# Encoder step on one core: a mixing paced anew, squares in another bank, copies on another engine, one evacuation behind two blocks

## The chip, the cores and the metric

The kernel runs on one core of a Trainium2 chip. The metric is device time in microseconds (us) of one execution; lower is better. TensorE multiplies matrices into PSUM banks; VectorE, ScalarE and GpSimd work on the data around it; SyncE issues most DMAs. In the profile TensorE is PE (its weight loads PEld), VectorE DVE, ScalarE ACT, GpSimd POOL, SyncE SP.

## The reference

One step of a streaming encoder with two layers for T = 1056 positions (1024 of a new stream, 32 of a running one) of width 1024, in float32. The even layer, which the change touches, reads:

```
h    = rms_norm(x, g_pre)
z    = h @ w_in                      # a | u | v | gate
y_a  = pool_mixer(a)                 # trailing means, a small matmul per group
v    = layer_norm(gelu(v));  u = gelu(u)
mix_ = W_s (128 x 128, masked, per head) applied over each chunk of 128 positions of v, + b_s
y_b  = u * mix_
y    = (concat(y_a, y_b) * silu(gate)) @ w_out
x    = x + rms_norm(y, g_post)
```

The odd layer starts with another rms_norm and a projection with w2, then does latent attention. The last piece of the change lies in that projection.

## The kernel before

Data lie transposed: 128 channels on the partitions, positions along the free axis. A tensor of 1024 channels is eight blocks. The 1056 positions are split into half a (640, computed as two pieces of 320 into a two-bank PSUM tile `za`) and half b (416, into a bank `zb`). Each float32 product is three matmuls of a rounded form (fp32r): high by high, high by low, low by high, in `mm_block` (L115). So each weight block has a high part, cast on ScalarE (L150), and a low part, the difference (L151, on GpSimd or VectorE), both made in `prep_w` from a raw block that SyncE loads; and each operand has such a pair. `za`, `zb` and `mi` have two buffers each, `whi` and `wlo` four, `raw` three.

The part that matters is the output projection of the even layer, in `even`. Its operand has sixteen blocks of channels: `mix[0..7]` (pool mixer times gate) and `mix[8..15]` (gating mixer times gate), the latter made from the tiles `mB[0..7]`, which lie in l8 to l15.

- First loop, m = 0 to 7: the product with `mix[0..7]`, half a for all m, half b only for m in BOTH = (0, 3, 4, 5). `put` (L678) copies the results to `yp[m]` with ScalarE (L679 from za, L681 from zb).
- While it runs, the mixing over positions goes on beside it. `sgu_task` starts nine tasks `sgu(t)`, one for each 128 positions. Each casts its piece of v (L743 on ScalarE, L744 on VectorE), and then for q = 0 to 3 sends a group of four small matmuls into an `mi` bank (in the trace `mi<-r,r`), reads it with VectorE (L763, L764, twice each) and multiplies the result into two blocks of mB with GpSimd (L766). Tiles 0 to 4 are half a.
- After the first loop, tasks are stepped until five tiles are done; then `split_a` (L781) casts the eight blocks of mB for half a: high part on ScalarE (L785), low part on VectorE (L786).
- Second loop, m = 0 to 7, half a: the product with `mix[8..15]`, added to `yp` (L827); the squares of the sum go into two banks (L831, ScalarE) and are summed up (L833, VectorE) for the norm that follows.
- Half b of w_out: twelve jobs in the order m = 6, 7, 1, 2 (two jobs each, low half and high half of the sixteen blocks), 0, 3, 4, 5 (one job each). The result is added to `yp[m].b` (L854) or, for 6, 7, 1, 2, copied there (L856); squares follow (L858, L860). The residual of half a runs beside it: `residual` (L863) with L884, L885, L896 on VectorE, L888 (a DMA), L895 and, for the squares, L289 on ScalarE and L290 on VectorE.
- `odd_in` (L911): w2 for half a in blocks 0 to 5, each followed by an evacuation on VectorE (`evac`, L192) that multiplies by rstd of half a's second norm; then half b. `rstd` (L198) sums over channels with small matmuls (L209), computes on VectorE (L216) and GpSimd (L217 to L219), spreads the result (L227, matmuls into `mi`, L240). For half b, L907 adds up the squares before it.

What sets the order: TensorE's order is the order of the program. Tasks are generators; each is due at a time of a pacing clock that advances by a fixed count with each matmul, and after each step over k `mm_block` takes one step of the task that is most overdue (`poll`). The table `N` (L35) holds the delays: "sg" ahead of the mixing's first task, "lead" from one tile to the next, "mix" between a tile's casts and its first group, "mixq" from group to group. The order on the other engines is made by a scheduler. The lines at the end of the first loop:

```
        while len(done) < 5:
            self.step(min(self.tasks, key=lambda t: t[:2]))
        split_a()
```

Of the kernel before, what the change touches and what calls it, by code (L numbers as in the profile page):

```python
# [23 lines left out]
NA, NB, CA = 640, 416, 320  # L24
# [7 lines left out]
        "kn e 2": 4.31, "v p 2": 5.302, "kn o 0": 6.344, "qn o 0": 6.796, "v p 3": 7.31, "v p 4": 8.3,  # L32
        "kn o 1": 8.827, "qn o 1": 10.546, "kn o 2": 12.035, "qn o 2": 12.785}

N = {"ld0": 18000, "ld": 8500, "tp": 5500, "sa": 9000, "sl": 12000, "sb": 6000, "sbk": 2000, "sg": 3000, "x": 462, "mix": 5000, "mixq": 2450, "tr": 717, "lead": 9800, "tr0": 11989, "res": 9194, "ra": 2699,  # L35
     "rb": 1574, "ha": 8000, "hb": 5000, "kv": 429, "q": 20908, "k": 34682, "kvs": 1773, "qs": 10662, "rest": 1357, "r1": 1608,
     "r2": 1337, "fa": 5400, "tn": 1800, "w0": 2000, "w1": 1552, "f0": 1645, "f1": 626, "fy": 648}
HF = 6
# [34 lines left out]
def two(ap):  # L73
    return ap.rearrange("p (c n) -> p c n", c=2)


class Build:
# [122 lines left out]
    def rstd(self, acc, g, dim, out, scale=None, wait=None):  # L200
# [14 lines left out]
        for w, c0, c1 in spans:  # L215
# [3 lines left out]
            nc.gpsimd.tensor_tensor(rl[:w, c0:c1], m[:w, c0:c1], rh[:w, c0:c1], ALU.subtract)  # L219
        yield (wait or (N["w0"], N["w1"]))[0]  # L220
        rep = None
        for c0 in range(0, len(widths), 2):
            ws = widths[c0 : c0 + 2]
            dh, dl = (self.t(self.cst, [P, 256], F32R, n) for n in ("dgh", "dgl"))
            for d, r in ((dh, rh), (dl, rl)):
                for e, w in enumerate(ws):
                    nc.vector.tensor_scalar(d[:w, e * P : e * P + w], self.ident[:w, :w], r[:w, c0 + e : c0 + e + 1],  # L227
                                            None, ALU.mult)
            yield (wait or (N["w0"], N["w1"]))[1]
            if c0 % 4 == 0:  # L230
# [88 lines left out]
    def even(self):  # L319
        nc = self.nc  # L320
# [27 lines left out]
        def split_x(g, k):  # L348
            x = xs[k][:, :NA] if g == "a" else xs[k][:, NA:T]
            hi, lo = h[k][0].get(g), h[k][1].get(g)  # L350
            nc.scalar.activation(hi, x, AF.Copy, scale=self.vec(GA1, k))
            nc.vector.scalar_tensor_tensor(lo, x, self.vec(GA1, k), hi, ALU.mult, ALU.subtract)
            return x
# [20 lines left out]
        def t_prep():  # L374
            for k in range(4):
                q = [[xs[k + 4 * i][:, j * HT : (j + 1) * HT] for j in range(2)] for i in range(2)]
                for i in range(2):
                    nc.scalar.activation(xs[k + 4 * i][:, :T], xs[k + 4 * i][:, :T], AF.Copy, scale=self.vec(GA1, k + 4 * i))
                tt = nc.vector.tensor_tensor
                tt(q[0][0], q[0][1], q[0][0], ALU.subtract)  # L380
                tt(q[0][1], q[1][1], q[0][1], ALU.subtract)
                tt(q[1][1], q[1][1], q[0][0], ALU.subtract)
                tt(q[1][0], q[1][0], q[1][1], ALU.subtract)
                for j, i in enumerate(((9, 10), (0, 4), (1, 5), (2, 6))[k]):
                    tl[2 * k + j] = R(i, F32R)
                for n, (j, e, o, f) in place.items():
                    hi, lo = X[n](k)
                    src = xs[k + o][:, f * HT : (f + 1) * HT]
                    nc.scalar.copy(hi, src)
                    tt(lo, src, hi, ALU.subtract)  # L390
                yield N["tp"]

# [6 lines left out]
        for g in "ab":  # L399
            acc, *sqs = (v[:, mpos[g]] for v in sums)  # L400
            z = [(zt[0], None), (zt[1], None)] if g == "a" else [(None, zt[2][:, i, :]) for i in range(2)]
            for k in range(NK):
                x = split_x(g, k)
                for i in range(2):
                    self.mm_block(self.wcol(wts[8 + i]), h, [k], g, ps=z[i], first=k == 0, last=k == 7)
                self.sumsq(acc, x, k == 0, g, nc.vector, sqs[k % 2])
            self.spawn(self.rstd(acc, g, D, rep.get(g)), N["x"])
            if g == "a":
# [78 lines left out]
        for g, z in (("a", zz), ("b", z)):  # L487
# [3 lines left out]
            if g == "a":  # L491
                tp = self.spawn(t_prep(), N["tp"])
            for i in range(2):
                ps = (zt[i], None) if g == "a" else (None, zt[2][:, i, :])
# [15 lines left out]
        def lead_task():  # L510

            for t in range(9):
# [12 lines left out]
                if t == 8:  # L525
                    w = R(13)
                    for e in range(2):
# [6 lines left out]
                        nc.scalar.dma_start(self.o_sv[:, o], lg)  # L534
                yield N["ld"]

# [24 lines left out]
        for p, (b0, b1) in enumerate(pairs):  # L561
# [13 lines left out]
            else:  # L575
                for e in range(2):
                    i = (b0, b1)[e] % 8
# [11 lines left out]
        mix = {}  # L589
# [12 lines left out]
        def pool_evac(blk, ps):  # L602
            a = pslot("a")
            nc.gpsimd.memset(a[:, 0:16], 0.0)
            nc.gpsimd.tensor_copy(a[:, 1040:1056], hist[:, blk, :])
            nc.vector.tensor_tensor(two(a[:, 16 : 16 + NA]), ps[0][:, :, :CA], two(rep.a), ALU.mult)
            nc.vector.tensor_tensor(a[:, 656:1040], ps[1][:, :384], rep.b[:, :384], ALU.mult)
            nc.vector.tensor_tensor(a[:, 1056:1088], ps[1][:, 384:NB], rep.b[:, 384:], ALU.mult)
            return a
# [40 lines left out]
        for i, blk in enumerate(A_ORDER):  # L650
# [5 lines left out]
            ps = self.mm_block(self.wcol(wts.pop(blk)), h, range(NK))  # L656
# [4 lines left out]
            a = pool_evac(blk, ps)  # L661
# [142 lines left out]
        for m in range(2, NK):  # L804
# [5 lines left out]
            ps = self.mm_block(self.wcol(w), mix, A_ORDER, "ab" if m in BOTH else "a")  # L810
# [7 lines left out]
        for m in range(NK):  # L818
            if m < 7:
                wn = self.prep_w(self.i_wout[m + 1, :, 1024:], lo_on=nc.vector)  # L820
            else:
                wA = self.prep_w(self.i_wout[6, :, :1024], lo_on=nc.vector)
            ps = self.mm_block(lambda k: self.wcol(wB)(k - 8), mix, range(8, 16), "a")
            if m < 7:
                wB = wn
            y = yp[m].a
            nc.vector.tensor_tensor(two(y), two(y), ps[0][:, :, :CA], ALU.add)  # L827
            for c in range(2):
                yc, ac = two(y)[:, c], two(acc)[:, c]
                sq = ac if m == 0 else self.bank("zb")[:, :CA]  # L830
                nc.scalar.activation(sq, yc, AF.Square)  # L831
                if m:
                    nc.vector.tensor_tensor(ac, ac, sq, ALU.add)  # L833
# [7 lines left out]
        for j, (m, c) in enumerate(jobs):  # L841
            if j + 1 < len(jobs):
                mm, cc = jobs[j + 1]
                wn = self.prep_w(self.i_wout[mm, :, cc * 1024 : cc * 1024 + 1024], lo_on=nc.vector)
            if c == 0:
                ps = self.mm_block(self.wcol(w), mix, A_ORDER, "b", last=False)
                w = wn
                continue
            ps = None if m in BOTH else ps
            ps = self.mm_block(lambda k: self.wcol(w)(k - 8), mix, range(8, 16), "b", ps=ps, first=ps is None)  # L850
            w = wn
            y = yp[m].b
            if m in BOTH:
                nc.vector.tensor_tensor(y, y, ps[1][:, :NB], ALU.add)  # L854
            else:
                nc.vector.tensor_copy(y, ps[1][:, :NB])  # L856
            sq = self.bank("za")[:, 0, :NB]
            nc.scalar.activation(acc if m == order[0] else sq, y, AF.Square)  # L858
            if m != order[0]:
                nc.vector.tensor_tensor(acc, acc, sq, ALU.add)  # L860
# [50 lines left out]
    def odd_in(self):  # L911
        nc = self.nc
# [3 lines left out]
        z = self.yp[:6]  # L916

        def block(i, groups, ps=None):
            w = wts.pop(i)
            if i + 1 < len(seq):  # L920
                wts[i + 1] = self.prep_w(self.i_w2[seq[i + 1]])
            return self.mm_block(self.wcol(w), h2, range(NK), groups, ps=ps)

        for b in range(6):
            ps = block(b, "a")
            while "a" not in self.reps or any(t is self.reps["a"] for t in self.tasks):
                self.step(min(self.tasks, key=lambda t: t[:2]))
            rep2 = self.rep2
            self.evac(ps, z[b], rep2, "a")
        while any(t is self.res for t in self.tasks):  # L930
            self.step(self.res)

# [2 lines left out]
        pss = [block(6 + b, "b", (None, zs[b])) for b in range(4)]  # L935
# [76 lines left out]
        for m in range(8):  # L1012
            ps = block(12 + m, "ab")
# [469 lines left out]
```

## Time and profile before

| | us |
|---|---|
| median of three runs | 1308.68 |
| lowest and highest | 1307.97, 1315.05 |
| profiled execution, its own time | 1318.26 |
| its span in the trace | 1316.2 |
| TensorE busy | 1265.5 (96%) |
| VectorE busy | 865.6 (66%) |
| ScalarE busy | 552.0 (42%) |
| GpSimd busy | 304.9 (23%) |

The profile is of one execution, slower by 9.6 us than the median. Positions in it are us from the start of its span. A timeline's row gives start, length, engine, line, operation, output <- inputs, shapes, the number of instructions taken together, and in brackets the idle time of the engine ahead of it with what ended that. Matmuls overlap, so from one to the next the starts are compared. [...]

### The profile page before, as it was taken

To read this page: it belongs to the slowest core of one execution; us is meant where nothing else is said; L and a number is where in the kernel's file an instruction comes from. 1 tells how busy PE (TensorE), PEld (TensorE's weight loads), DVE (VectorE), ACT (ScalarE), POOL (GpSimd) and SP (SyncE) were. 2 spreads that over 40 slices of the span, in tenths; PEclk is the share of its full clock that TensorE was granted. 3 is DMA by queue.
4 is the path that set the end of the run, shared out by engine and by line. 5 is a ranking of instruction groups with operands and counts; after the bars stand their busy time and mean duration, and the time that the engine had idled before them with its cause. 6 is when DMAs were issued, how large, how long until landed. Compare 5 with 4: busy or idle time off the path is not lost.

```text
span 1316.2 us, 22118 instructions
## 1 busy us (share of the span) xinstructions
PE 1265.5 (96%) x8488; PEld 1232.0 (94%) x8488; DVE 865.6 (66%) x1620; ACT 552.0 (42%) x1035; POOL 304.9 (23%) x381
## 2 busy tenths in 40 slices
PE   9899999999999999999998999999999999999995
PEld 8899989999999999989997989999999999998993
DVE  7977668886768764478578824733667666665438
ACT  8643432343422223243344423424556565654431
POOL 0200000000033332443102444222223332322410
PEclk9899999999999999989999989998999999999998
DMA  6022346522233253222355333222111111116425
GB/s 226 10 89 98 99 154 209 196 69 88 95 110 107 65 187 126 73 78 88 125 167 177 105 117 115 95 82 66 47 44 46 48 46 52 46 53 198 160 88 193
DMA packets 77562, 139.40 MB, mean 106 GB/s; under 512 B 10736, under 2 KB 33712, under 8 KB 77456
## 3 DMA queue, kind: packets, MB, share of 16 engines
q1 hardware_dynamic: 57776, 105.57, 25.5%
q10 hardware_dynamic: 19680, 32.42, 6.8%
q8 instruction: 67, 1.10, 0.3%
q14 instruction: 39, 0.32, 0.1%
HBM read 101.74 MB, written 36.21 MB: 105 GB/s over the span
## 4 chain that ended last, share of the span: by engine, by line
PE 79%; DVE 11%; DMA 4%; issue 3%; ACT 1%; POOL 1%; ACTq 0%; SPq 0%; DVEq 0%; POOLq 0%
PE za L115 20%; PE z L115 18%; PE sc L115 12%; PE pj L115 12%; PE zb L115 11%; PE pj L1157 2%; PE mi L115 2%; DMA r<-vd 1%; DVE wlo L447 1%; DMA r<-in_w 1%; PE mi L209 1%; DVE wlo L151 1%; PE mi L549 1%; DVE a L1380 1%; DVE r L907 1%
## 5 line engine op out<-in xcount | busy, mean ns | idle before, releaser
L115 PE MATMUL z<-l,whi 128*128 128x264 f32 (+2 forms) x1312 | 248.9, 296 | 9.6 <-DVE r L192 2.1
L150 ACT CAST whi<-raw 128x512 fp32r<-128x512 f32 (+1 forms) x180 | 108.3, 604 | 309.9 <-PE zb L115 134.9
L151 POOL TENSOR_TENSOR wlo<-raw,whi 128x512 fp32r<-128x512 f32 (+2 forms) x122 | 157.0, 1289 | 296.1 <-ACT whi L150 290.9
L115 PEld LDWEIGHTS z<-l,whi 128*128 128x128 f32 x1312 | 197.3, 191 | 12.9 <-DVE r L477 2.5
L115 PE MATMUL z<-l,wlo 128*128 128x264 f32 (+2 forms) x880 | 187.6, 292 | 2.6 <-DVE wlo L447 2.6
L115 PE MATMUL za<-a,whi 128*128 128x320 f32 x704 | 145.2, 313 | 0.9 <-DVE r L641 0.9
L115 PEld LDWEIGHTS z<-l,wlo 128*128 128x128 f32 x880 | 140.0, 191 | 3.2 <-DVE wlo L447 3.1
L115 PEld LDWEIGHTS za<-a,whi 128*128 128x128 f32 x704 | 117.4, 190 | 1.6 <-ACT whi L150 1.2
L115 PE MATMUL za<-l,whi 128*128 128x320 f32 (+1 forms) x496 | 112.2, 316 | 0.0
L115 PEld LDWEIGHTS za<-l,whi 128*128 128x128 f32 x496 | 90.8, 191 | 0.7
L1130 POOL TENSOR_SCALAR p<-p,nm 128x128 f32<-128x128 f32 (+8 forms) x72 | 53.0, 736 | 164.5 <-DVE nm L1129 129.1
L115 PE MATMUL z<-r,whi 128*128 128x264 f32 x448 | 90.6, 284 | 0.0
L115 PE MATMUL za<-a,wlo 128*128 128x320 f32 x352 | 80.6, 310 | 0.0
L115 PE MATMUL zb<-l,whi 128*128 128x416 f32 x224 | 76.4, 353 | 0.0
L115 PE MATMUL zb<-b,whi 128*128 128x416 f32 x224 | 72.4, 358 | 1.9 <-DVE rep L833 1.9
L1128 ACT ACTIVATE p<-sc,nm 128x128 f32<-128x128 f32 (+8 forms) x72 | 50.6, 703 | 45.1 <-DVE nm L1127 31.9
L115 PEld LDWEIGHTS z<-r,whi 128*128 128x128 f32 x448 | 69.3, 188 | 0.0
L446 ACT CAST whi<-r 128x512 fp32r<-128x512 f32 x56 | 34.7, 621 | 77.3 <-PE z L115 60.9
L115 PEld LDWEIGHTS za<-a,wlo 128*128 128x128 f32 x352 | 62.0, 190 | 0.2
L447 DVE TENSOR_TENSOR wlo<-r,whi 128x512 fp32r<-128x512 f32 x56 | 38.4, 685 | 30.5 <-ACT whi L446 30.5
L115 PE MATMUL za<-l,wlo 128*128 128x320 f32 (+1 forms) x248 | 58.1, 313 | 0.0
L115 PE MATMUL sc<-a,whi 128*128 128x400 f32 x256 | 57.6, 346 | 0.2 <-ACT p L1128 0.2
(317 smaller groups left out, 3049.5 us busy)
## 6 DMA issues: line engine op xcount, KB each, us to landing
raw<-in_w SPq DMA_DIRECT2D x64, 256.0 KB, 2.7
r<-in_w SPq DMA_DIRECT2D x56, 256.0 KB, 2.8
raw<-in_wout SPq DMA_DIRECT2D x56, 256.0 KB, 3.1
mBd<-r ACTq DMA_DIRECT2D x8, 528.0 KB, 2.8
gAd<-r ACTq DMA_DIRECT2D x8, 528.0 KB, 3.5
l<-mBd SPq DMA_DIRECT2D x8, 528.0 KB, 5.8
vd<-r ACTq DMA_DIRECT2D x16, 256.0 KB, 2.9
r<-vd SPq DMA_DIRECT2D x8, 512.0 KB, 4.3
```

What stands on the lines that cost most here:

```text
L115: self.nc.tensor.matmul(out, lhsT, rhs, start=start, stop=stop)
L150: nc.scalar.copy(hi[:, :m], raw[:, :m])
L151: (lo_on or nc.gpsimd).tensor_tensor(lo[:, :m], raw[:, :m], hi[:, :m], ALU.subtract)
L209: nc.tensor.matmul(st[:w, j : j + 1], acc[:, j * P : j * P + w], self.one, start=True, stop=True)
L446: nc.scalar.copy(hi, src)
L447: lo_on.tensor_tensor(lo, src, hi, ALU.subtract)
L549: nc.tensor.transpose(pt[:n, j * 256 + e * P : j * 256 + (e + 1) * P], d[e][:, i * P : i * P + n], self.ident)
L907: nc.vector.tensor_tensor(acc2, acc2, sq, ALU.add)
L1128: nc.scalar.activation(pv, view, AF.Exp, bias=nm[:n, 0:1], accum_out=nm[:n, 1:2])
L1130: nc.gpsimd.tensor_scalar(p[:n, :K], p[:n, :K], nm[:n, 2:3], 1.0, ALU.mult, ALU.mult)
L1157: nc.tensor.transpose(tr[:, e, :], p[:, (b + e) * P : (b + e + 1) * P], self.ident)
L1380: nc.vector.scalar_tensor_tensor(y[m], y[m], self.vec(GP2, m), rep, ALU.mult, ALU.mult)
```

## The change

Four edits. The pacing delays "sg", "mix" and "lead" are shorter. In the second loop's last block the squares of half a are written to the `mi` bank instead of `zb`. The copies of L856 are made by ScalarE. In `odd_in` the evacuation of block 0, and with it the loop that steps tasks until rstd is there, stands behind block 1 in the program.

```diff
--- before.py
+++ after.py
@@ -32,7 +32,7 @@
         "kn e 2": 4.31, "v p 2": 5.302, "kn o 0": 6.344, "qn o 0": 6.796, "v p 3": 7.31, "v p 4": 8.3,
         "kn o 1": 8.827, "qn o 1": 10.546, "kn o 2": 12.035, "qn o 2": 12.785}
 
-N = {"ld0": 18000, "ld": 8500, "tp": 5500, "sa": 9000, "sl": 12000, "sb": 6000, "sbk": 2000, "sg": 3000, "x": 462, "mix": 5000, "mixq": 2450, "tr": 717, "lead": 9800, "tr0": 11989, "res": 9194, "ra": 2699,
+N = {"ld0": 18000, "ld": 8500, "tp": 5500, "sa": 9000, "sl": 12000, "sb": 6000, "sbk": 2000, "sg": 0, "x": 462, "mix": 3200, "mixq": 2450, "tr": 717, "lead": 9000, "tr0": 11989, "res": 9194, "ra": 2699,
      "rb": 1574, "ha": 8000, "hb": 5000, "kv": 429, "q": 20908, "k": 34682, "kvs": 1773, "qs": 10662, "rest": 1357, "r1": 1608,
      "r2": 1337, "fa": 5400, "tn": 1800, "w0": 2000, "w1": 1552, "f0": 1645, "f1": 626, "fy": 648}
 HF = 6
@@ -827,7 +827,7 @@
             nc.vector.tensor_tensor(two(y), two(y), ps[0][:, :, :CA], ALU.add)
             for c in range(2):
                 yc, ac = two(y)[:, c], two(acc)[:, c]
-                sq = ac if m == 0 else self.bank("zb")[:, :CA]
+                sq = ac if m == 0 else self.bank("mi" if m == 7 else "zb")[:, :CA]
                 nc.scalar.activation(sq, yc, AF.Square)
                 if m:
                     nc.vector.tensor_tensor(ac, ac, sq, ALU.add)
@@ -853,7 +853,7 @@
             if m in BOTH:
                 nc.vector.tensor_tensor(y, y, ps[1][:, :NB], ALU.add)
             else:
-                nc.vector.tensor_copy(y, ps[1][:, :NB])
+                nc.scalar.copy(y, ps[1][:, :NB])
             sq = self.bank("za")[:, 0, :NB]
             nc.scalar.activation(acc if m == order[0] else sq, y, AF.Square)
             if m != order[0]:
@@ -921,12 +921,17 @@
                 wts[i + 1] = self.prep_w(self.i_w2[seq[i + 1]])
             return self.mm_block(self.wcol(w), h2, range(NK), groups, ps=ps)
 
+
+        pss = []
         for b in range(6):
-            ps = block(b, "a")
+            pss.append(block(b, "a"))
+            if b == 0:
+                continue
             while "a" not in self.reps or any(t is self.reps["a"] for t in self.tasks):
                 self.step(min(self.tasks, key=lambda t: t[:2]))
             rep2 = self.rep2
-            self.evac(ps, z[b], rep2, "a")
+            for i in (0, 1) if b == 1 else (b,):
+                self.evac(pss[i], z[i], rep2, "a")
         while any(t is self.res for t in self.tasks):
             self.step(self.res)
```

How instructions move. First TensorE, at the start of the second loop, in the kernel before; `mi_...` are groups of the mixing, `za_755` is block 0 of the second loop (another group, mi_739, stands directly ahead of these rows):

```order
L115 MATMUL mi_744_6205<-r5_638_5464,r1_722_6063 128x256
L115 MATMUL mi_744_6205<-r5_638_5464,r3_723_6064 128x128
L115 MATMUL mi_744_6205<-r5_638_5464,r1_722_6063 128x256
L115 MATMUL mi_744_6205<-r5_638_5464,r3_723_6064 128x128
L115 MATMUL mi_746_6217<-r5_638_5464,r1_722_6063 128x256
L115 MATMUL mi_746_6217<-r5_638_5464,r3_723_6064 128x128
L115 MATMUL mi_746_6217<-r5_638_5464,r1_722_6063 128x256
L115 MATMUL mi_746_6217<-r5_638_5464,r3_723_6064 128x128
L115 MATMUL za_755_6258<-r6_641_5471,whi_726_6083 128x320 x2
L115 MATMUL za_755_6258<-r7_642_5472,whi_726_6083 128x320 x2
```

Three groups stand back to back there, between block 7 of the first loop and block 0 of the second. The same place in the changed kernel, from the last matmul of block 7 (`za_739`) on:

```order
L115 MATMUL za_739_6142<-a6_616_5349,wlo_717_6016 128x320 x2
L115 MATMUL mi_747_6221<-r5_638_5464,r1_722_6033 128x256
L115 MATMUL mi_747_6221<-r5_638_5464,r3_723_6034 128x128
L115 MATMUL mi_747_6221<-r5_638_5464,r1_722_6033 128x256
L115 MATMUL mi_747_6221<-r5_638_5464,r3_723_6034 128x128
L115 MATMUL za_756_6263<-r6_641_5471,whi_734_6131 128x320 x2
L115 MATMUL za_756_6263<-r7_642_5472,whi_734_6131 128x320 x2
L115 MATMUL za_756_6263<-r6_641_5471,wlo_735_6132 128x320 x2
L115 MATMUL za_756_6263<-a0_469_4461,whi_734_6131 128x320 x2
L115 MATMUL za_756_6263<-a1_471_4463,whi_734_6131 128x320 x2
L115 MATMUL za_756_6263<-a0_469_4461,wlo_735_6132 128x320 x2
L115 MATMUL mi_758_6283<-r5_638_5464,r2_740_6161 128x256
```

One group is left between the blocks; mi_744 and mi_745 (a group of the sixth tile) now lie inside block 7, and mi_758, the sixth tile's second, inside block 0.

Next VectorE in the changed kernel, up to the last row that reads mi_745 (a... are the split blocks of `mix`, l12 and l13 blocks of mB, dgh, dgl and tm temporaries):

```order
L763 SCALAR_TENSOR_TENSOR dgh_746_6214<-mi_744_6180,vecs_5_69,r8_639_5469 128x128
L764 SCALAR_TENSOR_TENSOR dgh_746_6214<-mi_744_6180,vecs_5_69,dgh_746_6214 128x128
L786 TENSOR_TENSOR a7_524_4791<-l12_631_5445,a6_522_4789 128x640
L763 SCALAR_TENSOR_TENSOR tm_757_6276<-mi_745_6203,vecs_5_69,r8_639_5469 128x128
L786 TENSOR_TENSOR a1_563_5051<-l13_632_5446,a0_561_5049 128x640
L764 SCALAR_TENSOR_TENSOR tm_757_6276<-mi_745_6203,vecs_5_69,tm_757_6276 128x128
L151 TENSOR_TENSOR wlo_755_6259<-raw_753_6257,whi_754_6258 128x512
L763 SCALAR_TENSOR_TENSOR dgl_748_6226<-mi_747_6221,vecs_5_69,r8_639_5469 128x128
L763 SCALAR_TENSOR_TENSOR tm_757_6276<-mi_745_6203,vecs_5_69,r8_639_5469 128x128
L764 SCALAR_TENSOR_TENSOR dgl_748_6226<-mi_747_6221,vecs_5_69,dgl_748_6226 128x128
L763 SCALAR_TENSOR_TENSOR dgl_748_6226<-mi_747_6221,vecs_5_69,r8_639_5469 128x128
L764 SCALAR_TENSOR_TENSOR tm_757_6276<-mi_745_6203,vecs_5_69,tm_757_6276 128x128
```

The reads of mi_744, mi_745 and mi_747 now stand among L786 of `split_a` and two L151 of the weights; before, the L151 stood behind all L786.

Last, ScalarE in the changed kernel, around the copy of the fourth of the blocks that L856 copies (l2; l5 is half a's residual):

```order
L888 DMA x1d_6_74<-l5_597_5228 128x640
L895 ACTIVATE a2_954_7416<-l5_597_5228,vecs_5_69 128x640
L289 ACTIVATE a8_896_7121<-l5_597_5228 128x640
L856 COPY l2_594_5225<-zb_943_7343 128x416
L150 CAST whi_958_7436<-raw_957_7435 128x512
L858 ACTIVATE za_956_7432<-l2_594_5225 128x416
L150 CAST whi_961_7442<-raw_960_7441 128x512
```

and VectorE in the kernel before, at the same copy:

```order
L290 TENSOR_TENSOR a7_895_7120<-a7_895_7120,a8_896_7121 128x640
L885 TENSOR_TENSOR l5_597_5228<-l5_597_5228,a5_893_7118 128x640
L856 COPY l2_594_5225<-zb_943_7343 128x416
L151 TENSOR_TENSOR wlo_959_7437<-raw_957_7435,whi_958_7436 128x512
L151 TENSOR_TENSOR wlo_962_7443<-raw_960_7441,whi_961_7442 128x512
L884 SCALAR_TENSOR_TENSOR l6_598_5229<-l6_598_5229,vecs_5_69,a6_894_7119 128x640
```

The copy stood behind L885 of l5 on VectorE; it now stands on ScalarE behind L895 and L289 of l5.

From TensorE's L209 of the second norm of half a on, no instruction of any engine changes its place against another of the same engine; that holds for all blocks of `odd_in`.

## Rows read from the trace of the kernel before

**Rows 1.** The page, part 1: busy us, share of the span, instructions.
```profile
PE 1265.5 (96%) x8488; PEld 1232.0 (94%) x8488; DVE 865.6 (66%) x1620; ACT 552.0 (42%) x1035; POOL 304.9 (23%) x381
```

**Rows 2.** TensorE's waits, 480 to 800 us: operand or bank awaited, total, times, longest.
```profile
PE mi L209 <- DVE r L907: 5.2, 1, 5.2
PE zb L115 <- DVE rep L833: 1.9, 1, 1.9
PE mi L115 <- DVE tm L764: 1.8, 1, 1.8
PE zb L115 <- DVE l L854: 1.6, 2, 1.3
PE mi L115 <- DVE dgh L764: 1.4, 1, 1.4
PE mi L115 <- DVE dgh L227: 1.1, 1, 1.1
PE mi L115 <- DVE dgl L227: 1.0, 1, 1.0
PE zb L115 <- DVE l L856: 1.0, 1, 1.0
```

**Rows 3.** Stretches: length, busy us of PE, PEld, DVE, ACT, POOL, granted clock, DMA.
```profile
580.00:586.00 6.00, 5.94 (x24) 5.97 (x25) 5.70 (x11) 3.99 (x6) 2.50 (x5) 0.52 0.03 11
597.00:647.00 50.00, 50.00 (x346) 49.12 (x346) 38.83 (x96) 18.11 (x34) 12.53 (x28) 1.00 0.24 67
650.00:654.00 4.00, 3.98 (x13) 3.81 (x14) 0.36 (x1) 0.13 (x1) 0.00 (x0) 0.57 1.04 397
671.00:711.00 40.00, 37.38 (x193) 35.27 (x192) 37.91 (x57) 22.37 (x36) 1.99 (x1) 1.00 0.68 213
760.00:766.30 6.30, 6.19 (x25) 6.16 (x26) 2.64 (x9) 0.74 (x1) 1.92 (x6) 0.50 0.41 145
```

**Rows 4.** TensorE's timeline, 566 to 576: start us, us, engine, line, what.
```profile
567.21 0.75 PE L115 MATMUL za<-a,whi 128*128 128x320 f32 x4
...
568.09 0.57 PE L115 MATMUL mi<-r,r 128*128 128x256 f32 x4
568.50 0.80 PE L115 MATMUL za<-a,whi 128*128 128x320 f32 x4
...
575.63 0.57 PE L115 MATMUL mi<-r,r 128*128 128x256 f32 x4
```

**Rows 5.** VectorE's timeline at the end of the mixing.
```profile
577.37 0.81 DVE L786 TENSOR_TENSOR a<-l,a 128x640 fp32r<-128x640 f32 x1
...
579.31 0.34 DVE L764 SCALAR_TENSOR_TENSOR dgh<-mi,vecs,dgh 128x128 f32<-128x128 f32 x1
579.57 0.34 DVE L764 SCALAR_TENSOR_TENSOR tm<-mi,vecs,tm 128x128 f32<-128x128 f32 x1
...
581.73 1.04 DVE L786 TENSOR_TENSOR a<-l,a 128x640 fp32r<-128x640 f32 x1
```

**Rows 6.** VectorE's timeline at the end of the second loop.
```profile
642.12 0.68 DVE L151 TENSOR_TENSOR wlo<-raw,whi 128x512 fp32r<-128x512 f32 x1
642.72 0.88 DVE L833 TENSOR_TENSOR rep<-rep,zb 128x320 f32<-128x320 f32 x2
```

**Rows 7.** GpSimd's timeline at the end of the mixing.
```profile
577.52 0.97 POOL L766 TENSOR_TENSOR l<-l,dgh 128x128 f32<-128x128 f32 x1 [1.42 <-DVE dgh L764]
...
581.63 0.46 POOL L766 TENSOR_TENSOR l<-l,dgh 128x128 f32<-128x128 f32 x1 [1.03 <-DVE dgh L764]
```

**Rows 8.** ScalarE's timeline there.
```profile
582.54 0.73 ACT L785 CAST a<-l 128x640 fp32r<-128x640 f32 x1
```

**Rows 9.** VectorE's timeline in half b of w_out.
```profile
695.03 0.59 DVE L856 COPY l<-zb 128x416 f32<-128x416 f32 x1
695.53 0.69 DVE L151 TENSOR_TENSOR wlo<-raw,whi 128x512 fp32r<-128x512 f32 x1
```

**Rows 10.** ScalarE's timeline in the first loop of w_out.
```profile
509.31 0.51 ACT L681 COPY l<-zb 128x416 f32<-128x416 f32 x1
```

## The prediction

> **What bounds the kernel now.** The busy table comes first: TensorE is busy 96% of the span, every other engine 66% or less [rows 1]. So the end is set by TensorE's own work and by the holes in it, and an edit that leaves the matmuls alone can only take holes away or make new ones. The list of TensorE's waits between 480 and 800 us, which covers all that the change touches, is therefore read next [rows 2]: each row is a hole, with the instruction that ended it. [...]
>
> [...]
>
> **A**, the end of the mixing over positions: 1.4 + 1.8 = 3.2 us of waiting for L764 [rows 2], then 6 us at a mean clock of 0.52 [rows 3]. Work that goes at 0.52 for 6 us would have taken 3.1 us, so the tail costs 2.9. Together 6.1.
>
> **B**, before half b of w_out: 1.9 us for L833 [rows 2], then 4 us at 0.57, a tail of 0.43 x 4 = 1.7. Together 3.6.
>
> **C**, inside half b of w_out: 1.0 us for L856 and 1.6 for L854 [rows 2] = 2.6. Their stretch was granted 1.00 [rows 3], so there is no tail.
>
> **D**, rstd of half a's second norm: 1.1 and 1.0 us for L227 [rows 2].
>
> **E**, rstd of half b's second norm: 5.2 us for L907 [rows 2] and a tail of 0.5 x 6.3 = 3.2. It is the largest, 8.4 us, and the change's last rows on each engine lie well ahead of it; I leave it as it is.
>
> **Edit 1, the pace of the mixing (place A).** Before, the last three groups of `mi` matmuls stand back to back behind block m=7 (first order fence). There are two `mi` buffers, so the second and third each wait until VectorE has read an older one: that is A. In the change three groups move into the blocks, and one more (tile 5's first) goes ahead of the second loop; behind block 7 only mi_747 is left, and mi_758 comes after two steps over k of the second loop's block 0 (second fence).
>
> TensorE's side: a step takes 568.09 - 567.21 = 0.88 us and a group 568.50 - 568.09 = 0.41 [rows 4]. Before, block 7 ended at 575.63 [rows 4]; with three more groups ahead of that it ends at 575.63 + 3 x 0.41 = 576.86. mi_747 takes it to 577.27, and after two steps, at 579.03, mi_758 is wanted.
>
> VectorE's side: mi_758 takes over the buffer of mi_745, which is free when the last row of the third fence has read it. In VectorE's order, from the first read of mi_744 (three rows ahead of that fence) up to there, stand 11 of L763/L764, 2 of L786 and 2 of L151. L763 and L764 follow each other at 579.57 - 579.31 = 0.26, an L786 takes 0.81 [rows 5], an L151 642.72 - 642.12 = 0.60 [rows 6]: 2.86 + 1.62 + 1.20 = 5.7 us. The run begins when mi_744 is there, four steps and one group before 576.86, at 572.93, and two L786 in front of it are done, 1.62 later: 574.55. One hole lies in it: the first L786 needs its l12 multiplied on GpSimd (0.46 us [rows 7]) and cast on ScalarE (0.73 [rows 8]) after an L764, 1.2 us in which VectorE has two rows (0.52) to do: 0.7 idle. The end is 574.55 + 5.7 + 0.7 = 580.95, with a semaphore's 0.1 about 581.1. So mi_758 **waits 2.1 us**. No row shows this wait, so it is bounded: 0 if VectorE comes into block 7 with no arrears, and about 3.2 (the whole of A's present waiting) if its L786 are stretched. I take 2.1, by the walk. A wait of 1.9 had a tail of 1.7 at B, and waits of 1.0 to 1.3 had none at C [rows 2, 3]; 2.1 is nearest to B, so I add 1.7. A comes to 3.8 in place of 6.1: **-2.3 us**.
>
> All nine tiles start earlier as well. From 597 to 647, VectorE is busy 38.83 of 50 us [rows 3], so it has room and I price that at 0; if it has none, see the last rival.
>
> **Edit 2, m=7's squares (place B).** Both zb buffers hold squares of the last block, and half b's first block waits for L833, the last reader. With the squares in `mi` it needs the zb of block 6's squares, read by the L833 at 642.72 [rows 6], seven us earlier. Its weights' last low part is L151 at 642.12 [rows 6]; nothing else is late. `mi` has no other user until the next rstd, in half b's third job, so the other bank costs nothing. Wait and tail go: **-3.6 us**. Next late would be the weights of the job after, which are cast as soon as this one gives its buffers back, and so move with it.
>
> **Edit 3, four copies to ScalarE (place C).** From 671 to 711 VectorE is busy 37.91 of 40 us [rows 3]: there it is the bound, some 5 us behind TensorE, and each zb buffer comes free when VectorE gets to it. A copy occupies it from 695.03 to 695.53, 0.50 us [rows 9]. Four that leave bring all behind them forward by **2.0 us**, and TensorE with them; the rest of C's 2.6, about 0.6, stays as smaller waits for L854. ScalarE takes 0.51 us for such a copy out of zb (the same in put()) [rows 10], at 22.37 of 40 busy [rows 3]: hidden. But its order matters: the copy of l2 stands behind L895 and L289 of l5 (fourth fence), which themselves wait for VectorE's L885 of l5. That row stands a few places earlier now, so I expect the copy done by about 694. TensorE wants the buffer 1.0 us [rows 2] before the copy of today ends (695.03 + 0.59), at 694.6. Bounds: 0 if it is late all the same, 2.6 if all three waits go.
>
> **Edit 4, block 0's evac.** TensorE's rstd rows already lay inside block 0, and on every engine the instructions of odd_in stand in the same sequence as before: the edit does not do what its code says, and I give it 0 from both sides. **D** keeps its 2.1: GpSimd's order ahead of that rstd is the same; one of its two waits, 1.1, may go or come again, and I use that for the range.
>
> **Sum.** -2.3 - 3.6 - 2.0 = -7.9 us, against the profiled execution's own 1318.26: 1310.4. That execution is 9.6 us above the median shown, 1308.68, with the same program; I take the difference over unchanged: **1300.8**.
>
> **Rivals.**
> (1) *A goes clean.* VectorE is ahead, mi_758 waits under 1 us, no tail. For it: VectorE was only 66% busy overall. Against it: 5.7 us of VectorE's work must fit in the 4.5 us from 574.55 to 579.03. -6.1 - 3.6 - 2.0 = -11.7: 1297.0.
> (2) *A is given back whole.* Where an L786 started beside GpSimd's L766 (581.63) it took 1.04 us in place of 0.81, and where GpSimd started second (577.52) its L766 took 0.97 in place of 0.46 [rows 5, 7]. Denser mixing makes such meetings more frequent. Five L786 in the walk times 0.23 = 1.2 more waiting: 3.3 with A's present tail of 2.9 is 6.2, against 6.1 now. The sum is then -5.6: 1303.1. [...]
> (3) *C gives nothing.* The copy of l2 comes out no earlier, since L885 of l5 is held in VectorE's queue: -2.3 - 3.6 = -5.9: 1302.8. With (2) as well: -3.6, 1305.1.
> (4) *Slower: the second loop cannot hold the new pace.* A tile comes every 9.0 in place of 9.8 of the pacing clock. If VectorE is full there, each of three later tiles waits like A now, 2.1 + 2.9 = 5.0: 15 in place of 6.1, +8.9 - 5.6 = +3.3: 1312.0. It decides once VectorE's share of the loop passes 100%; it is 78% now [rows 3], and 78 x 9.8/9.0 is 85. That speaks against it.
> (5) *An edit does nothing.* For edit 4 that is part of the forecast.
>
> **How the numbers follow.** Forecast 0.50; (1) 0.16; (2) 0.16; (3) 0.10; (4) 0.05; others 0.03. A measurement of this kernel can tell about 0.5%, 6.5 us, from no change: the line is at 1302.1. The forecast is 1.3 us below it, with errors of 1 to 2, so a quarter of its chance counts as no change: 0.37 and 0.13. Faster: 0.37 + 0.16 + 0.03 of (2) = 0.56. Same: 0.13 + 0.13 of (2) + 0.10 + 0.02 = 0.38. Slower: 0.05 + 0.01 = 0.06. The range goes from (1) with all of C (1296.4) less one wait of D, 1295.3, to (2) and (3) together, 1305.1, plus one wait of D, 1306.2.
>
> **What would show it.** A wait of about 2 us of an `mi` matmul for L764 in the second loop's block 0, with a granted clock near 0.5 behind it, in place of the two ahead of the loop; no wait for L833, and a clock of 1.00 where half b starts; zb waits between 690 and 712 under 1 us in sum; the waits for L227 and L907 as before, the last still 5 us with its tail. Wrong would be: new waits in the second loop (rival 4), an unchanged wait for l2's copy, now on ScalarE (3), or a changed E, which I hold fixed.

## The result and the profile after

| | before | changed |
|---|---|---|
| median, us | 1309.62 (4 runs) | 1301.99 (4 runs) |
| lowest to highest | 1307.97 to 1315.05 | 1299.84 to 1302.51 |
| span of the profiled execution | 1316.2 | 1298.0 |

The ratio of the changed kernel's time to the other's is 0.9922, 95% interval 0.9899 to 0.9945: 10.2 us off 1309.6, between 7.2 and 13.2. The medians in the table are 7.6 apart, inside that interval. The prediction was -7.9 us, 1300.8 with a range of 1295.3 to 1306.2, and faster at 0.56.

The spans differ by 18.2 us, more than the medians, since they are single executions. The traced one of the changed kernel is the fastest of its four (mean granted clock, as a share of TensorE's full clock, 0.991; the others 0.987 to 0.989 and 1.9 to 2.7 us longer), and that of the kernel before, 1318.26 us, is slower than every run in the table. So a stretch is cut out that both traces share: it begins at the `za` matmul that waits 0.9 us for L641, shortly ahead of the first row that the change moves, and ends at half b's L209, behind the last. First the kernel before, then the changed one, TensorE's timeline:

```profile
500.21 0.82 PE L115 MATMUL za<-a,whi 128*128 128x320 f32 x4 [0.89 <-DVE r L641]
```

```profile
760.11 1.64 PE L209 MATMUL mi<-one,r 128*128 128x1 f32 x8 [5.19 <-DVE r L907]
```

```profile
496.23 0.82 PE L115 MATMUL za<-a,whi 128*128 128x320 f32 x4 [0.88 <-DVE r L641]
```

```profile
746.41 1.63 PE L209 MATMUL mi<-one,r 128*128 128x1 f32 x8 [5.20 <-DVE r L907]
```

From start to start that is 259.90 us before and 250.18 in the changed kernel: **9.7 us** gone inside the stretch. The rest, 4.0 ahead of it and 4.5 behind, lies where nothing was changed.

TensorE's waits in the changed kernel, 480 to 800 us, as in [rows 2]:

```profile
PE mi L209 <- DVE r L907: 5.2, 1, 5.2
PE mi L115 <- DVE tm L764: 2.2, 1, 2.2
PE mi L115 <- DVE dgl L227: 1.0, 1, 1.0
...
PE zb L115 <- DVE wlo L151: 0.3, 1, 0.3
PE mi L115 <- DVE dgh L227: 0.3, 1, 0.3
PE zb L115 <- ACT whi L150: 0.2, 1, 0.2
PE mi L115 <- DVE dgh L764: 0.2, 1, 0.2
```

The two waits of A have become one of 2.2 and one of 0.2, L833 (B) is gone, no wait for L854 or L856 is left (C), only 0.3 and 0.2 for weights; L907 (E) stands as it was. The stretches, columns as in [rows 3]:

```profile
576.00:580.00 4.00, 1.93 (x14) 1.96 (x15) 4.00 (x10) 1.46 (x3) 3.14 (x4) 1.00 0.21 66
580.00:586.00 6.00, 6.00 (x45) 6.00 (x44) 5.77 (x14) 2.36 (x5) 1.85 (x4) 1.00 0.45 131
...
640.00:650.00 10.00, 10.00 (x55) 9.88 (x55) 4.30 (x7) 3.45 (x7) 0.00 (x0) 1.00 0.85 293
...
746.40:752.70 6.30, 6.29 (x30) 6.26 (x31) 2.54 (x8) 1.34 (x2) 1.91 (x6) 0.62 0.38 133
```

The 2.2 us end at 578.07, and the stretches around it and behind were granted 1.00: no tail, as a stretch of lower clock behind a wait is called, at A, where [rows 3] had 0.52 for 6 us. Half b's start, at 640.7, has 1.00 as well. VectorE did not become idle in half b of w_out: from half b's first matmul to half a's L209 it is busy 46.56 of 57.45 us, against 46.74 of 61.47 before; the four copies are gone from it, and a few rows that lay ahead of it or behind it have come in. Behind E the clock is still low, 0.62 in the mean.

The last rows of the third order fence as they ran, on VectorE, and the matmul that they release:

```profile
571.41 0.34 DVE L763 SCALAR_TENSOR_TENSOR dgh<-mi,vecs,r 128x128 f32<-128x128 f32 x1
...
573.95 0.83 DVE L786 TENSOR_TENSOR a<-l,a 128x640 fp32r<-128x640 f32 x1 [0.69 <-ACT a L785]
...
574.95 0.81 DVE L786 TENSOR_TENSOR a<-l,a 128x640 fp32r<-128x640 f32 x1
...
577.58 0.34 DVE L764 SCALAR_TENSOR_TENSOR tm<-mi,vecs,tm 128x128 f32<-128x128 f32 x1
```

```profile
578.07 0.65 PE L115 MATMUL mi<-r,r 128*128 128x256 f32 x4 [2.21 <-DVE tm L764]
```

From the first read of mi_744 (571.41) to the end of the last of mi_745 (577.92) it took 6.5 us, 0.69 of it idle for ScalarE's cast; the walk through VectorE's rows in the prediction had 5.7 + 0.7. The matmul starts 0.15 us behind that end, where the walk had 0.1 for the semaphore. ScalarE around the fourth copy:

```profile
682.14 0.83 ACT L895 ACTIVATE a<-l,vecs 128x640 fp32r<-128x640 f32 x1 [1.59 <-DVE wlo L151]
682.87 0.72 ACT L289 ACTIVATE a<-l 128x640 f32<-128x640 f32 x1
683.50 0.48 ACT L856 COPY l<-zb 128x416 f32<-128x416 f32 x1
```

L895 and L289 of l5 do stand in front of it; it ends at 683.98, and TensorE, which needs that bank next, starts at 684.56 after a wait of 0.22 us for weights. Their cast (L150, 683.89 to 684.51) is the row behind the copy on ScalarE.

### The profile page after: what moved, and what is told of

It reads as the page before. It is cut to its first block, busy times and chain, and to the rows that moved or that the text cites. A ratio compares the mean times of both kernels' runs of the same rounds, so it can differ in the third digit from the quotient of the medians.

```text
span 1298.0 us, 22126 instructions
## 1 busy us (share of the span) xinstructions
PE 1255.4 (97%) x8488; PEld 1222.3 (94%) x8488; DVE 862.1 (66%) x1616; ACT 552.5 (43%) x1039; POOL 306.4 (24%) x381
## 4 chain that ended last, share of the span: by engine, by line
PE 79%; DVE 11%; DMA 4%; issue 3%; ACT 2%; POOL 1%; ACTq 0%; SPq 0%; DVEq 0%; POOLq 0%
PE za L115 20%; PE z L115 18%; PE sc L115 12%; PE pj L115 11%; PE zb L115 11%; PE pj L1162 2%; PE mi L115 2%; DMA r<-vd 1%; DVE wlo L447 1%; DVE wlo L151 1%; PE mi L209 1%; PE mi L549 1%; DVE r L907 1%; DVE a L1385 1%; DVE l L884 1%
## 5 line engine op out<-in xcount | busy, mean ns | idle before, releaser
L150 ACT CAST whi<-raw 128x512 fp32r<-128x512 f32 (+1 forms) x180 | 107.9, 603 | 290.1 <-PE zb L115 121.2
L151 POOL TENSOR_TENSOR wlo<-raw,whi 128x512 fp32r<-128x512 f32 (+2 forms) x122 | 157.8, 1296 | 289.0 <-ACT whi L150 285.4
```

Source lines behind the costliest of these rows:

```text
L150: nc.scalar.copy(hi[:, :m], raw[:, :m])
L151: (lo_on or nc.gpsimd).tensor_tensor(lo[:, :m], raw[:, :m], hi[:, :m], ALU.subtract)
```

## The experiments

The first four start from the changed kernel and put back one edit each. Ratios are to the kernel before, as timed on the same chip; the changed kernel has 0.9922, and the one with block 0's evacuation put back, which runs the same, 0.9911, so 0.9917 is taken for it. Worked out from the two intervals, that is known to about 0.0013, so a run that differs from it by less than some 0.0025 is not told apart by the ratio alone. One thousandth is 1.3 us. "The stretch" is the one from the wait for L641 to half b's L209, 250.18 us in the changed kernel.

### The pacing put back

```diff
-"sg": 0,  "mix": 3200,  "lead": 9000
+"sg": 3000,  "mix": 5000,  "lead": 9800
```

> The changed kernel with the three pacing delays put back to those of before; the other edits stay. My theory, each place pays for itself: the two waits for L764 between the loops come back (1.4 and 1.8 us) in place of the one of 2.2 in block 0, with a tail of about 2.9 us behind them, no wait for L833, none over 0.5 us in half b of w_out. Against the changed kernel +2.3 us if that one's wait has its tail in most executions, up to +3.9 if it has none: a ratio to the kernel before of about 0.995. Rival, the later stretch absorbs it: VectorE is the bound in half b of w_out, so what comes early from the mixing waits there; then the ratio stays at 0.992 and zb waits in half b shrink by as much as the start is late.

Measured: 1303.42 us, ratio 0.994 (0.992 to 0.996). TensorE's waits and the granted clock:

```profile
PE mi L115 <- DVE tm L764: 1.8, 1, 1.8
PE mi L115 <- DVE dgh L764: 1.4, 1, 1.4
```

```profile
576.00:580.00 4.00, 3.82 (x16) 3.85 (x17) 3.71 (x9) 3.66 (x6) 1.65 (x4) 0.57 0.02 9
```

Both waits are back to the tenth, with a tail, though a shorter one: 0.43 x 4 = 1.7 us, where the kernel before lost 2.9. The stretch takes 252.17 us, 2.0 more; by the ratio it is 0.0023, 3.0 us, about as much as the ratio can tell. The early start is not absorbed later: half b's waits are for weights only (0.5 and 0.3).

### The last squares back in zb

```diff
-sq = ac if m == 0 else self.bank("mi" if m == 7 else "zb")[:, :CA]
+sq = ac if m == 0 else self.bank("zb")[:, :CA]
```

> The changed kernel with the last squares back in zb. My theory: a wait of about 1.9 us for L833 at the start of half b of w_out comes back, with a tail at half clock of about 1.7 us: +3.6 us, a ratio to the kernel before of about 0.995. The rest is as in the changed kernel, so its wait of 2.2 us in block 0 is a second look at whether that wait has a tail: by the length of the wait alone it should have one (1.9 had one), and did not in the one trace seen. Rival, the later stretch absorbs it: +0 to +1, ratio 0.992 to 0.993.

Measured: 1304.85 us, ratio 0.9942 (0.9929 to 0.9955), 3.3 us more than the changed kernel.

```profile
PE zb L115 <- DVE rep L833: 1.9, 1, 1.9
```

```profile
642.00:646.00 4.00, 3.73 (x19) 3.65 (x20) 1.22 (x3) 0.67 (x2) 0.00 (x0) 1.00 1.03 394
```

The wait for L833 is back with its 1.9 us, but in this trace without a tail: 1.00 from 642 on, where [rows 3] had 0.57 behind the same wait. The stretch is 1.7 us longer. So of B's 3.6 us about 1.9 is sure, and 1.7 a tail that one trace has and another has not. The wait of 2.2 us in block 0 is there too, without a tail again (1.00 from 576 to 590).

### The copies back on VectorE

```diff
-nc.scalar.copy(y, ps[1][:, :NB])
+nc.vector.tensor_copy(y, ps[1][:, :NB])
```

> The changed kernel with the four copies back on VectorE. My theory, VectorE is the bound there and each copy costs 0.50 us of it: the zb waits in half b of w_out (0 for VectorE's L854 and L856 now, 2.6 us before) come back to 2.0 to 2.6 us: ratio to the kernel before about 0.994. Rival, the copies were not what cleared that stretch, but the earlier start or the other order of VectorE's rows: then the waits stay under 1 us in sum and the ratio is 0.992.

Measured: 1305.41 us, ratio 0.9949 (0.993 to 0.9967), 4.2 us more.

```profile
PE mi L115 <- DVE dgh L227: 1.4, 1, 1.4
PE mi L115 <- DVE dgl L227: 1.0, 1, 1.0
PE zb L115 <- DVE l L854: 1.0, 2, 0.7
...
PE zb L115 <- DVE l L856: 0.5, 1, 0.5
```

```profile
708.00:712.00 4.00, 2.96 (x12) 2.90 (x12) 2.33 (x7) 0.00 (x0) 0.77 (x1) 0.62 0.46 131
```

The waits in half b come back to 1.5 us, less than expected; to half a's L209 that costs 1.2 us. The larger part lies behind: two waits for L227, 2.5 together, and a tail of 0.38 x 4 = 1.5. The stretch is 3.5 us longer. What happened at L227 is in VectorE's and GpSimd's timelines:

```profile
706.08 1.54 DVE L227 TENSOR_SCALAR dgh<-ident,rh 128x128 fp32r<-128x128 f32 x2 [2.75 <-POOL rh L218]
707.55 1.50 DVE L227 TENSOR_SCALAR dgl<-ident,sm 128x128 fp32r<-128x128 f32 x2
...
709.46 0.47 DVE L227 TENSOR_SCALAR dgh<-ident,rh 128x128 fp32r<-128x128 f32 x2
```

```profile
706.28 2.49 POOL L151 TENSOR_TENSOR wlo<-raw,whi 128x512 fp32r<-128x512 f32 x2
```

A pair of L227 takes 1.5 us while GpSimd works on L151, and 0.47 a little later. The same two engines in the changed kernel:

```profile
704.61 1.51 DVE L227 TENSOR_SCALAR dgh<-ident,rh 128x128 fp32r<-128x128 f32 x2
```

```profile
704.69 2.58 POOL L151 TENSOR_TENSOR wlo<-raw,whi 128x512 fp32r<-128x512 f32 x2 [1.74 <-ACT whi L150]
```

There GpSimd waits 1.74 us for a cast before it begins this L151; the first two pairs are through by then, and the two after them meet it. Here and in the kernel before GpSimd goes on to L151 without a pause, and the first two meet it (before: L151 at 716.50, the first two pairs from 716.30 on, 1.55 and 1.50 us). TensorE waits for the first two at once, so there both cost it something, and in the changed kernel 0.3 and 1.0.

### Block 0's evacuation put back

```diff
-        pss = []
-        for b in range(6):
-            pss.append(block(b, "a"))
-            if b == 0:
-                continue
+        for b in range(6):
+            ps = block(b, "a")
...
-            for i in (0, 1) if b == 1 else (b,):
-                self.evac(pss[i], z[i], rep2, "a")
+            self.evac(ps, z[b], rep2, "a")
```

> The changed kernel with block 0's evacuation back in front of block 1. My theory: nothing moves on any engine that matters, ratio to the kernel before 0.992, the waits of 1.0 us for L227 and 5.2 us for L907 as they are. Rival, the edit took away a wait: the wait for L227 of 1.1 us that the changed kernel shows shrunk to 0.3 comes back, ratio 0.993. It is also a third look at the tail behind the wait of 2.2 us.

Measured: 1299.86 us, ratio 0.9911 (0.9896 to 0.9927); the stretch takes 250.00 us, against 250.18, and the waits of 5.2 us for L907, 2.2 for L764 and 1.0 for L227 stand as they were.

No effect can be seen, as the forecast had it for this edit (rival 5).

### The copies alone

The kernel before with the third edit and no other.

> The kernel before with nothing but the four copies on ScalarE. Putting them back cost the changed kernel 3.5 us in its trace: 1.2 in half b of w_out, and 2.3 at the rstd behind it (waits for L227 of 1.45 and 1.0 us with a short tail, against 0.25 and 1.0). My theory, VectorE's 2.0 us carry it and it stands by itself: the three zb waits of 2.6 us shrink to under 1, ratio to the kernel before 0.997 to 0.9985. Rival, it needs the earlier start that the other edits give: ratio 1.000, waits of 2 us or more stay. The wait for L833 and those between the loops (1.4 and 1.8) are as before; whether each has its tail is another sample.

Measured: 1306.77 us, ratio 0.9959 (0.9944 to 0.9975), 5.4 us faster than before.

```profile
PE zb L115 <- DVE rep L833: 1.9, 1, 1.9
...
PE mi L115 <- DVE dgl L227: 1.0, 1, 1.0
...
PE zb L115 <- ACT whi L150: 0.6, 1, 0.6
```

```profile
578.00:582.00 4.00, 4.00 (x20) 4.00 (x19) 4.00 (x8) 2.39 (x5) 1.88 (x3) 0.61 0.00 0
...
645.00:649.00 4.00, 3.67 (x12) 3.56 (x13) 0.67 (x2) 0.11 (x1) 0.00 (x0) 0.62 1.04 404
```

It stands by itself, and with more than the 2 to 4 us expected; its stretch, 255.97, is 3.9 us shorter than before's, of which 1.0 had come by half b's first matmul, where the difference to be seen is a shorter tail at A. By its trace, then, some 2.9 are the copies' own. The waits for L854 and L856 are gone without any earlier start, and of those for L227 one is left. A and B have their waits as before, and tails, 0.61 and 0.62 for 4 us.

### The sixth tile later

The changed kernel, with

```diff
-                yield N["lead"]
+                yield N["lead"] + (2400 if t == 4 else 0)
```

> The changed kernel with the sixth tile of the mixing started 2400 ns of the pacing clock later, so that its first group comes after two steps of the second loop's block 0 and its second after six, instead of inside block 7 and after two. My theory, the wait of 2.2 us in block 0 is there because VectorE has 5.7 us of work between mi_744 and the last read of mi_745: now those reads end with the fifth tile, the wait goes or stays under 0.5 us, no tail; -2.2 us against the changed kernel, ratio to the kernel before about 0.990 (the changed one: 0.9911 and 0.9922 in two comparisons). Rival, VectorE's arrears of the splits stay and the next group meets them: a wait of 1 to 2 us at the sixth tile's second group, ratio 0.9915.

Measured: 1302.01 us, ratio 0.9918 (0.9894 to 0.9942).

```profile
583.11 0.56 PE L115 MATMUL za<-a,whi 128*128 128x320 f32 x2 [0.15 <-ACT a L785]
583.97 0.56 PE L115 MATMUL za<-a,whi 128*128 128x320 f32 x2 [0.30 <-DVE a L786]
```

The wait of 2.2 us is gone; in its place the block's own operands are late by 0.15 and 0.30, since the casts of `split_a` now come just in time. From the wait for L641 to half b's first matmul it is 142.65 us, against 144.47 in the changed kernel: 1.8 off. The ratio's interval is 6 us wide and does not show it by itself.

### The second norm's rstd of half b later

```diff
-"hb": 5000
+"hb": 11000
```

> The changed kernel with rstd of half b's second norm due 11000 instead of 5000 ns of the pacing clock after its sums are issued: its small matmuls stand seven steps over k (6.2 us) later in TensorE's order, at the end of w2's block 5 instead of after one step of it. My theory, the wait for L907 of 5.2 us and its tail at half clock, about 3 us, are only there because TensorE reaches that row too early: both go, and the evacuations of half b, which need this rstd, come four blocks (18 us) later and do not wait: -8 us, ratio to the kernel before about 0.9855. Rival, it moves the wait: half b's evacuations wait for the later rstd and the wait for L194 in the blocks behind (2.0 us now) grows by up to 6 us: gain 2 or less, ratio 0.990.

Measured: 1297.77 us, ratio 0.9895 (0.9871 to 0.992). TensorE's waits, and GpSimd and VectorE at the place:

```profile
PE mi L115 <- DVE dgh L227: 2.2, 1, 2.2
PE mi L115 <- DVE dgl L227: 2.2, 2, 1.1
```

```profile
748.47 2.68 POOL L151 TENSOR_TENSOR wlo<-raw,whi 128x512 fp32r<-128x512 f32 x2 [3.87 <-ACT whi L150]
751.11 1.36 POOL L217 TENSOR_TENSOR sm<-sm,mhalf 128x3 f32<-128x3 f32 x2
```

```profile
752.64 1.68 DVE L227 TENSOR_SCALAR dgh<-ident,rh 128x128 fp32r<-128x128 f32 x2 [3.05 <-POOL rh L218]
754.24 1.81 DVE L227 TENSOR_SCALAR dgl<-ident,sm 128x128 fp32r<-128x128 f32 x2
```

The wait for L907 is gone, but neither theory had what came: 2.2 and 1.15 us for the L227 that spread the result (the row of 2.2 in two has one of 1.0 that was there before), with a granted clock of 0.50 behind them from 756 to 764. L217 stands on GpSimd behind two L151, and both pairs of L227 take 1.7 and 1.8 us beside GpSimd. The wait moved within the rstd, not to the evacuations. By the ratio, 2.9 us of the 8 hoped for, about as much as the ratio can tell.

### Both, and then longer pauses inside rstd

Both delays in one kernel:

> Both of the two delays in one kernel. If each does what my theory says, -10 us against the changed kernel: ratio to the kernel before about 0.984, some 1290 us. If both rivals hold, 0.990 or above.

Measured: 1295.42 us, ratio 0.9875 (0.9852 to 0.9899), half of what was expected. In its trace the two L227 wait 2.1 and 1.2 us again, here with 2.5 us of matmuls between them and a clock of 1.00 from 748 to 760. So for half b's second norm the two pauses of `rstd`, between its sums and the spreading and between the pieces of that, were made longer:

```diff
-self.rstd(acc2, g, D, self.rep2.get(g))
+self.rstd(acc2, g, D, self.rep2.get(g), wait=(4400, 2600) if g == "b" else None)
```

> The kernel with both delays, and the two pauses inside rstd of half b's second norm longer (4400 and 2600 instead of 2000 and 1552 ns of the pacing clock): the matmuls that spread its result stand some seven steps over k (4 us) later. Moving the small matmuls alone took away the wait for L907 of 5.2 us, and put waits for L227 of 2.2 and 1.2 us in its place, since GpSimd's L217 stands behind two L151 and L227 then meets the next. My theory: with 4 us more these two go as well and nothing waits in their place, -3.3 us and a tail where there was one: ratio to the kernel before about 0.985. Rival, the evacuations of half b come too late and their zb buffers hold up block 10: a wait for L194 of 2 us or more, ratio 0.987 or above.

Measured: 1293.46 us, ratio 0.9859 (0.9839 to 0.988).

```profile
PE mi L115 <- DVE dgl L227: 1.7, 2, 1.0
```

```profile
740.00:760.00 20.00, 19.16 (x114) 18.53 (x113) 13.95 (x19) 4.88 (x8) 14.16 (x16) 1.00 0.50 165
```

Of those 1.7, 1.0 is half a's, so 0.7 is left where 5.2 stood, with a clock of 1.00 there and on to 790, and TensorE waits nowhere up to 800 for L194. The same for half a as well, with pauses of 3000 and 2600:

> As the one with the longer pauses for half b, and longer pauses for half a's second norm too (3000 and 2600): the waits for L227 of 1.0 us, and of 0.3 in some traces, ahead of block 0's evacuation should go: -1 us more, ratio 0.984. Rival: the evacuations of w2's blocks 0 and 1 come later by some 5 us, block 2 waits for its bank (a wait for L192 of 1 us or more), and the gain is 0 or a loss.

Measured: 1291.7 us, ratio 0.985 (0.9826 to 0.9874).

```profile
PE za L115 <- DVE l L192: 3.1, 1, 3.1
```

The rival came: the waits for L227 are gone, and block 2 of w2 waits 3.1 us for the evacuation of block 0. By the waits that is a loss of 1.4 us, by the ratio the two kernels cannot be told apart. Both are faster than the changed kernel, by some 7 to 9 us.

## Why the prediction was right, step by step

**A, the pace: -2.3 forecast, -3.7 in this trace** (waits of 3.2 us to 2.4, and the tail of 2.9). The wait of 2.1 us at mi_758 came as 2.21, at the place and for the instruction named. VectorE's run took 6.5 us where the walk had 6.4. Both sides were some 0.8 us later than the walk put them (with the 4.0 us added by which the changed trace is ahead there), which left the difference as it was. The step that failed is "2.1 is nearest to B, so I add 1.7": the wait had no tail in the five traces that hold it (the changed kernel, the two with the squares and the copies back, the one with block 0's evacuation back, the one with rstd of half b later). Whether the other executions of the changed kernel had a tail there is open. Put back, the pacing costs 2.0 us of the stretch and 3.0 by the ratio, so -2.3 lies within what the runs tell.

**B, the squares: -3.6 forecast.** 1.9 of it is the wait, and returned to the tenth. The 1.7 of tail was taken from one execution as if it were fixed; of three traces with this wait, each of another kernel, two have it and one has not. With the squares back the ratio gives 3.3.

**C, the copies: -2.0 forecast, 1.2 of the stretch up to half a's L209 when put back.** The mechanism was right: no wait for L854 or L856 is left, and 0.5 us for weights took their place, 2.1 off where 2.0 was forecast. With the copies back, 1.5 of the 2.6 came again, and no wait for weights.

**D: 0 forecast, 1.1 kept for the range, and the reason given was wrong.** "D keeps its 2.1: GpSimd's order ahead of that rstd is the same" argued from the order, and the order was not the point. In the traces, which L227 meets which L151 goes by when the two come, and that shifted: 1.3 us of waiting in place of 2.1, and with the copies back 2.5 and a tail. In the two traces where the first L227 meets L151 it also starts later behind half a's L209, by 4.8 us (before) and 5.2 (copies back) against 4.6. Together with the 1.2 of C this makes the copies worth 3.5 us in the trace and 4.2 by the ratio, nearly twice the 2.0 of the sum. The statement that no instruction changes its place from that L209 on is wrong by one row: VectorE's L854 of the last job now stands between the first two L227, where before it stood ahead of both. No run put that row back alone.

**E and edit 4** stayed as said: 5.2 us with a tail, and nothing.

The rivals: (1), A clean, came halfway, a full wait without a tail. (2), the splits stretched by GpSimd, did not show where it would have cost: the L786 in the run took 0.83 and 0.81 us. The two just behind the run took 2.02 together, and TensorE waited for neither. What such a meeting costs shows at L227 instead: 1.5 us for a pair beside L151, 0.47 without; no run here took the L151 away to show it by itself. (3) did not come: the copy of l2 ended before its bank was wanted. (4) did not come: over the whole second loop, 573.9 to 640.7, TensorE has no wait of 0.2 us or more but the one of 2.2, and VectorE is busy 50.21 of 66.8 us.

The sum against the trace, part by part: the stretch is cut at half b's first matmul and at half a's L209, before and changed.

```profile
650.02 0.66 PE L115 MATMUL zb<-b,whi 128*128 128x416 f32 x2 [1.91 <-DVE rep L833]
...
711.47 1.17 PE L209 MATMUL mi<-one,a 128*128 128x1 f32 x10
```

```profile
640.70 0.54 PE L115 MATMUL zb<-b,whi 128*128 128x416 f32 x2
...
698.15 1.17 PE L209 MATMUL mi<-one,a 128*128 128x1 f32 x10
```

Of the 9.7 us, 5.3 went ahead of the first cut, 4.0 between the two and 0.4 behind. The forecast has 4.2 in the first part (A, and B's wait), 3.7 in the second (B's tail, and C) and nothing in the third. So the mechanisms carry the result, and the misses, 1.1 at A, 0.3 and 0.4, are all on the same side: the sum, -7.9, was too small, and the measured -10.2 (7.2 to 13.2) agrees. Luck has a part in the number itself: the tails were priced from one execution, so what they are worth in the median is not shown.

## What to carry to other kernels

Where one engine is the end and its order is fixed, its holes can be priced one by one from the list of waits, and a new one foreseen by counting what the engine it waits for has to do in between. Price what comes behind a hole separately: the low clock after it is there in one trace and not in another (behind the wait of 1.9 us for L833, 0.57 over 4 us in one and 1.00 in another). And where an engine's rows take longer beside those of another, as a pair of L227 did beside GpSimd's L151 (1.5 us, 0.47 without), an unchanged order does not keep a wait as it is: with the first two pairs through before L151 began, TensorE waited 0.3 and 1.0 us for L227, and 1.4 and 1.0 where they met it. For a wait at the end of a chain of such rows, moving its reader later, with longer pauses inside the chain, took 4.5 us off the largest wait (5.2 to 0.7), which no edit of the change touched.

## What the runs showed of the hardware

TensorE's clock behind a wait is not set by that wait's length alone. The wait of 1.91 us for L833 was followed by 0.57 over 4 us in the kernel before, by 0.62 with the copies alone, and by 1.00 with the squares back. The wait of 2.2 us in block 0 had 1.00 behind it in all five traces; two waits of 1.4 and 1.8 us with one small group between them had a tail in all three (before, pacing back, copies alone), of 2.9, 1.7 and 1.6 us. With half b's rstd later, 2.2 and 1.15 us with one matmul between them were followed by 0.50 for some 8 us; with both delays, 2.1 and 1.2 us with 2.5 us of matmuls between them had 1.00. Behind the wait of 3.1 us for L192 in the last run, longer than any of these, two steps over k took 0.88 us each (716.98 to 718.74), as in [rows 4], where the clock was 1.00. What decides between them was not tried out and stays open.

On VectorE, the seven L907 of half b took 0.6 us apiece just ahead of GpSimd's L151 and after it, and 1.5 to 1.7 beside it (three in 4.81), in the changed kernel; a pair of L227 took 1.5 in place of 0.47. TensorE waits 5.2 us for the end of the chain of L907, the longest of its waits from 480 to 800.
